# Hybrid decoder layer on one core: one more projection group in seven products, tighter pairs of heads, and 72 convolution taps moved from VectorE to ScalarE and DMAs

## The chip, the cores and the metric

The kernel runs on one core of a Trainium2 chip. The metric is the device time of one execution in microseconds (us). The engines are called as the profile calls them: PE (TensorE, matrix products), DVE (VectorE), ACT (ScalarE), POOL (GpSimd) and SP (SyncE, which here only issues DMAs). Each engine executes its own instructions strictly in the order in which they stand in the program, and waits where an instruction's inputs or its output buffer are not ready.

## The reference

One layer on a sequence of 512 tokens with 2048 channels. The input is normalised and multiplied with a matrix of 7168 columns; the columns feed a causal convolution of 31 taps (mixer A) and an attention with three dilated windows (mixer B); both results are gated and multiplied with the output matrix.

```python
h = rms_norm(x, norm_g)
z = h @ w_in                       # (512, 2048) @ (2048, 7168)
a_val, a_glu, a_gate, q, k, v, b_gate = jnp.split(z, SPLIT_POINTS, axis=-1)

u = a_val * jax.nn.sigmoid(a_glu)
u = causal_depthwise_conv(u, conv_w, conv_b)           # 31 taps
u = jax.nn.silu(layer_norm(u, conv_norm_g, conv_norm_b))
u = u @ conv_pw_w + conv_pw_b
y_a = u * jax.nn.silu(a_gate)

q = rms_norm(q.reshape(bsz, s, N_HEADS, HEAD_DIM), q_norm_g)
k = rms_norm(k.reshape(bsz, s, N_HEADS, HEAD_DIM), k_norm_g)
o = dilated_attention_mixture(q, k, v)
y_b = o.reshape(bsz, s, ATTN_WIDTH) * jax.nn.silu(b_gate)

y = jnp.concatenate([y_a, y_b], axis=-1) @ w_out
return x + y
```

## The kernel before, in words

**Groups, units and slots.** The columns of the matrices are cut into groups of 512. `GROUPS` (line 49) lists them in the order in which PE works on them: four groups `vg` (value and gate of the convolution's GLU), then `q`, `k`, `v`, `bg` (gate of mixer B) of the first eight heads, `q`, `k`, `v` of the other eight, `ag` twice (gate of mixer A), the second `bg`, the convolution's projection `pw` twice, and the output groups `wb` and `wa`. A group's weights come in units of 1 MB (four blocks of 128 rows by 512 columns); a group of the input matrix has four units, a group of `pw` two. The time of the program is counted in slots, eight to a unit; `clock[0]` is the number of the slot that is being written. `vg` 0 to 3 fill slots 0 to 127, `q` 0 slots 128 to 159, `k` 0 slots 160 to 191, the two groups after it slots 192 to 255, `q` 1, `k` 1 and `v` 1 slots 256 to 351, `ag` slots 352 to 415, the second `bg` slots 416 to 447, `pw` slots 448 to 479.

**Three products for one.** Values are kept at higher than fp16 accuracy by splitting each into two fp16 parts. A weight unit of a plain group is split by ACT (`split_hi`, line 297, tile `wh`) and DVE (`split_lo`, line 305, tile `wl`), and each product is three matmuls, high by high, high by low, low by high (`tri`, lines 411 to 415). A plain slot is six matmuls with 512 columns. In a unit with the number i, the `wh` of unit i+1 is issued in its first slot and the `wl` in its third. The pool `parts` holds two units' `wh` and `wl`, so the `wh` of unit i+1 overwrites that of unit i-1 and cannot start before PE has read the last of that unit, at the start of unit i.

**Seven products for eight.** The groups in `SEVEN` (line 54) are done with Winograd's form of Strassen's scheme: the weights and the activations are cut into two by two blocks and seven block products take the place of eight (`input_products`, line 1119, with `ORDER`, line 1116). Such a group has 28 product steps of twelve matmuls with 256 columns in the place of its 32 slots. Block sums of the weights are made by DMAs that POOL issues with `accum_op=add` (line 1134) and by DVE subtractions; each block is split by ACT (`hi`, line 1136) and DVE (`lo`, line 1140); the block products are recombined by ACT copies and DVE additions (`copy`, `joint`, `fourth`, `out`).

**Banks.** The pool `lin_ps` holds four PSUM banks (`LP`, line 32). A plain group uses them for its four row blocks m = 0 to 3. Block m is emptied right after it is done, in slots 1, 3, 5 and 7 of the group's last unit; the next group opens its own block m in slots 0, 2, 4, 6 of its first unit, in the bank of the same m. A gate group (`ag`, `bg`) is emptied by ACT with a Silu (`evac_gate`, line 460).

**The convolution.** `conv` (line 544) works on eight tiles `cv` in pairs. ACT starts each with tap 30 and the bias (line 551), and DVE adds the 30 other taps, each one instruction `cv<-u,cw,cv`. These are fillers: after each slot `run_conv` (line 861) adds DVE instructions of the convolution as long as the counted load of DVE is under a pace per slot (`PACE`, `PACE_2`, in estimated nanoseconds). The sum `lnacc` over the eight tiles, for the LayerNorm's mean, is added up pair by pair as they finish. Three slots after the last addition, PE multiplies it with ones (line 575) and the rest of the LayerNorm follows; its Silu (line 608) and the split of the result into `u16` (line 315) are ACT's.

**Attention.** `attention` (line 800) starts a pair of heads every `PERIOD` slots, eight pairs in all, and `two_heads` (line 706) has the plan of a pair, in slots after its start: scores on PE at 0 and 3, the exponentials of the first head by ACT at 7 and of the second at 11 (`exps`, line 741), their normalised high parts by ACT at 13 and 18 (`high`, line 749) and low parts by DVE at 16 and 21, DMA transposes at 19 and 24, and the products with `v` on PE when the pair ends. With `PERIOD` 32 the eight pairs begin in slots 226, 258, 290, 322, 354, 386, 418 and 450.

**Tables.** ACT needs an `ACT_TABLE_LOAD` when it goes from Exp to Silu or Sigmoid and back; the other functions here (Copy, Identity, Square) need none.

## Time and profile before

| what | us |
|---|---|
| median of 3 runs (815.09 to 815.63) | 815.55 |
| the profiled execution's own time | 815.08 |
| its span, first to last instruction | 813.3 |
| PE busy in it | 806.7 |
| DVE busy | 703.3 |
| ACT busy | 557.5 |
| POOL busy | 132.2 |

The granted TensorE clock was 1.00 over the whole span. The difference between span and time, 1.8 us, lies around the program. A row of the timeline gives start and duration in us, engine, line, operation, tiles and shape; an idle time before it and what ended it stand in brackets. A row such as `x4` merges neighbours. Consecutive instructions of one engine overlap a little (DVE and ACT by 0.08 to 0.1 us, PE by more, since matmuls are pipelined), so the cost of one in a queue is the distance from its start to the next one's start.

### The profile page before, as it was taken

The page shows a single profiled execution, that of the slowest core. Times are in us where ns is not written, and L with a number is a line of the kernel's source. Part 1 is how long each engine was busy: PE and PEld are TensorE (multiplying, and loading weights), DVE is VectorE, ACT ScalarE, POOL GpSimd, SP SyncE. Part 2 cuts the span into 40 slices and gives each one's busy share as a digit, 9 for nine tenths or more (in the row PEclk, how much of TensorE's full clock was granted, in tenths as well). Part 3 has the DMA queues.
Part 4 walks back from the last instruction along what each step waited for, and adds up shares of the span by engine and source line. Part 5 has one row for each costly group of instructions (what it writes and reads, how often), then busy time and mean ns, then how long its engine had stood idle before and what let it go on. Part 6 is the DMA issues. An engine that isn't in the chain of part 4 may idle for free.

```text
span 813.3 us, 13452 instructions
## 1 busy us (share of the span) xinstructions
PE 806.7 (99%) x5271; PEld 500.9 (62%) x5271; DVE 703.3 (86%) x1188; ACT 557.5 (69%) x784; POOL 132.2 (16%) x143
## 2 busy tenths in 40 slices
PE   9999999999999999999999999999999999999998
PEld 6887745888646854444444444444444444788887
DVE  6768999878989989999999989997678798998885
ACT  6667687577756688586757658497688858766540
POOL 0001021322224300004012010000110002412420
PEclk9999999999999999999999999999999999999999
DMA  9852346983874863527474623526352487678752
GB/s 339 329 235 99 109 102 138 142 249 58 311 146 104 149 263 108 122 95 169 142 182 127 150 100 107 123 95 169 104 121 100 137 246 226 118 176 187 130 105 65
DMA packets 98367, 125.60 MB, mean 154 GB/s; under 512 B 62464, under 2 KB 83712, under 8 KB 89088
## 3 DMA queue, kind: packets, MB, share of 16 engines
q1 hardware_dynamic: 80544, 107.37, 42.2%
q0 software_dynamic: 17472, 17.30, 15.0%
q8 instruction: 41, 0.67, 0.3%
q14 instruction: 22, 0.18, 0.1%
q10 hardware_dynamic: 288, 0.07, 0.0%
HBM read 88.56 MB, written 4.19 MB: 114 GB/s over the span
## 4 chain that ended last, share of the span: by engine, by line
PE 90%; DVE 7%; ACT 1%; issue 1%; POOL 0%; DMA 0%; SPq 0%; ACTq 0%; DVEq 0%
PE ps_l L413 24%; PE ps_l L415 23%; PE ps_l L414 23%; PE ps_l L887 10%; DVE cv L81 3%; PE ps_s L413 2%; PE ps_s L415 2%; PE ps_s L414 2%; PE ps_s L730 2%; PE ps_o L771 2%; DVE wl L81 1%; DVE ws L81 1%; ACT junk L191 0%; DVE sx L81 0%; DMA x<-xt_dram 0%
## 5 line engine op out<-in xcount | busy, mean ns | idle before, releaser
L81 DVE SCALAR_TENSOR_TENSOR cv<-u,cw,cv 128x511 f32<-128x511 f32 (+14 forms) x240 | 162.1, 727 | 0.4 <-ACT cv L551 0.4
L191 ACT ACTIVATE junk<-wf 128x2048 uint8<-128x2048 f32 x68 | 129.1, 1899 | 2.4 <-DMA wf<-w_dram 2.1
L300 ACT ACTIVATE wh<-wf,ws 128x2048 f16<-128x2048 f32 x44 | 87.7, 1994 | 52.4 <-PE ps_l L414 50.6
L413 PE MATMUL ps_l<-x,wh 128*128 128x512 f16 x320 | 121.3, 379 | 0.3 <-DVE glu L81 0.3
L415 PE MATMUL ps_l<-x,wl 128*128 128x512 f16 x320 | 121.3, 379 | 0.0
L414 PE MATMUL ps_l<-x,wh 128*128 128x512 f16 x320 | 121.3, 379 | 0.0
L81 DVE SCALAR_TENSOR_TENSOR wl<-wf,ws,wh 128x2048 f16<-128x2048 f32 x45 | 105.6, 2346 | 10.7 <-ACT wh L300 10.7
L413 PE MATMUL ps_l<-wh,x 128*128 128x512 f16 x256 | 97.1, 379 | 0.0
L415 PE MATMUL ps_l<-wh,x 128*128 128x512 f16 x256 | 97.0, 379 | 0.0
L414 PE MATMUL ps_l<-wl,x 128*128 128x512 f16 x256 | 97.0, 379 | 0.0
L81 DVE SCALAR_TENSOR_TENSOR ws<-wf,ws 128x1024 f16<-128x1024 f32 x70 | 89.0, 1278 | 7.1 <-ACT ws L1138 4.5
L413 PEld LDWEIGHTS <-wh 128*128 128x128 f16 x480 | 47.0, 98 | 55.3 <-issue 4.0
L415 PEld LDWEIGHTS <-wl 128*128 128x128 f16 x480 | 46.9, 98 | 53.6 <-DVE wl L81 0.4
L414 PEld LDWEIGHTS <-wh 128*128 128x128 f16 x480 | 46.9, 98 | 50.4 <-issue 0.7
L887 PE MATMUL ps_l<-xr,wr 128*128 128x512 f32 x288 | 69.6, 397 | 0.7 <-ACT xr L338 0.7
L205 POOL TENSOR_SCALAR ws<-ws 128x1 f32<-128x1 f32 x22 | 11.8, 537 | 324.4 <-DVE ws L81 295.6
L887 PEld LDWEIGHTS ps_l<-xr,wr 128*128 128x128 f32 x288 | 53.8, 188 | 14.3 <-ACT xr L338 1.5
L413 PEld LDWEIGHTS <-x 128*128 128x128 f16 x352 | 34.4, 98 | 32.5 <-issue 1.9
L415 PEld LDWEIGHTS <-x 128*128 128x128 f16 x352 | 34.4, 98 | 31.3
L414 PEld LDWEIGHTS <-x 128*128 128x128 f16 x352 | 34.4, 98 | 30.1
L954 ACT ACTIVATE ws<-wf,ws 128x1024 f16<-128x1024 f32 x28 | 32.1, 1147 | 28.3 <-PE ps_l L415 9.7
L1138 ACT ACTIVATE ws<-wf,ws 128x1024 f16<-128x1024 f32 x42 | 47.1, 1138 | 5.8 <-PE ps_l L415 4.8
(251 smaller groups left out, 1816.3 us busy)
## 6 DMA issues: line engine op xcount, KB each, us to landing
wf<-w_dram SPq DMA_DIRECT2D x72, 1024.0 KB, 5.2
wf<-wf POOLq DMA_DIRECT2D x30, 512.0 KB, 6.5
x<-xt_dram SPq DMA_DIRECT2D x16, 256.0 KB, 6.7
res<-xt_dram SPq DMA_DIRECT2D x8, 512.0 KB, 6.6
out_dram<-res SPq DMA_DIRECT2D x15, 256.0 KB, 2.2
wf<-w_dram SPq DMA_DIRECT2D x7, 512.0 KB, 7.2
wf<-wf POOLq DMA_DIRECT2D x6, 256.0 KB, 6.3
wf<-w_dram SPq DMA_DIRECT2D x2, 256.0 KB, 3.1
```

The source lines that it names most:

```text
L81: return getattr(self.engine, name)(out, src, *args, **kw)
L191: A.activation(junk[:, :n], src, AF.Square, scale=scale, accum_out=acc)
L205: G.tensor_scalar(scale, scale, 1e-30, 2.0 ** (-2 * top), op0=OP.max, op1=OP.mult)
L300: A.activation(parts[i][0], raw[i], AF.Copy, scale=wscale[units[i][3:]][0])
L413: T.matmul(ps, ah, bh, start=first, stop=False, skip_group_check=more)
L414: T.matmul(ps, ah, bl, start=False, stop=False, skip_group_check=more)
L415: T.matmul(ps, al, bh, start=False, stop=last, skip_group_check=more)
L730: T.matmul(ps[i, a], qk["q", hf][p4 // 2][rows, p4 % 2, q, i * P:w], qk["k", hf][p4 // 2][rows, p4 % 2, k, :w], start=n == 0, stop=n == 2)
L771: T.matmul(po[rows, i * P:(i + 1) * P], vs[hf][j // 2][:, j % 2, 2 * p4 + a, vp * DH:(vp + 1) * DH], got["t", a][:, pp * (ALL // P) + FROM ...
L887: T.matmul(banks[group, m], wt[:, a, m * P:(m + 1) * P], xk[b], start=k == 0 and a == b == 0, stop=k == KC - 1 and a == 1)
L954: A.activation(t[:, 0], block(name), AF.Copy, scale=wscale["wa", g][0])
L1138: A.activation(t[:, 0], block(name, pair), AF.Copy, scale=wscale[group][0])
```

## The change

1. `bg` 0 stands in front of `v` 0 in `GROUPS`, and is one of the groups in seven products. `input_products` gets a branch that empties such a gate group with Silu.
2. A pair of heads starts every 28 slots instead of 32, and the first 60 slots after `k` 0 instead of 28. The eight pairs now begin in slots 258, 286, 314, 342, 370, 398, 426 and 454. The plan of a pair is shorter: exponentials at 7 and 10, high parts at 11 and 15, low parts at 13 and 17, transposes at 16 and 20.
3. For three of the four pairs of `cv` tiles, 13 of the 31 taps (the starting one and 12 more) are made by ACT into a tile `tap` (two buffers) and summed in DRAM by DMAs that POOL issues with `accum_op=add`, one tap every three slots from slot 70 on, but none while `q` 0 is worked on. When the last has been sent, SP fetches the sum as the start of `cv`, and DVE adds the 18 other taps. So DVE has 72 tap instructions fewer (240 to 168), ACT 72 more, and POOL issues 78 tap DMAs and 6 more block sums for `bg` 0.
4. `lnacc` is added up in one piece, seven additions, when all eight tiles are done. The paces are 1180 and 1370 instead of 1230 and 1480. The pool `slots` has 33 buffers instead of 35.

```diff
-PERIOD = {0: 32, 1: 32}
+PERIOD = 28
-PACE = 1230
+BY_SUMS = {2: 12, 4: 12, 6: 12}
+STEP = 3
+SUMS_FROM = 70
+SLOW = (("q", 0),)
+PACE = 1180
-GROUPS = [... ("q", 0), ("k", 0), ("v", 0), ("bg", 0), ("q", 1), ...
+GROUPS = [... ("q", 0), ("k", 0), ("bg", 0), ("v", 0), ("q", 1), ...
-SEVEN = (("vg", 3), ("q", 0), ("v", 0))
+SEVEN = (("vg", 3), ("q", 0), ("bg", 0), ("v", 0))
-PACE_2 = 1480
+PACE_2 = 1370
+    taps = pool("taps", 2)
+    scratch = pool("scratch", 6, space=bass.MemoryType.DRAM)
+    def tap_sums():
+        for i0, count in BY_SUMS.items():
+            while i0 + 1 not in u:
+                yield 1
+            for i in (i0, i0 + 1):
+                far_sums[i, "at"] = scratch.tile([P, S], F32, name="far")
+            for d in range(count + 1):
+                for i in (i0, i0 + 1):
+                    t = taps.tile([P, S], F32, name="tap")
+                    scale = cw[:, i, TAPS - 1 - d:TAPS - d]
+                    if d == 0:
+                        A.activation(t, u[i], AF.Identity, scale=scale, bias=cb[:, i:i + 1])
+                    else:
+                        A.activation(t[:, d:], u[i][:, :S - d], AF.Copy, scale=scale)
+                    after(1, lambda: nc.gpsimd.dma_start(far_sums[i, "at"][:, d:], t[:, d:],
+                                                         **({"accum_op": OP.add} if d else {})))
+                    yield STEP
+                    while at_group[0] in SLOW:
+                        yield 1
+            far_sums[i0] = far_sums[i0 + 1] = clock[0] + 6
     def conv():
         for i0 in range(0, 8, 2):
+            far = BY_SUMS.get(i0, 0)
+            while far and far_sums.get(i0 + 1, 10 ** 9) > clock[0]:
+                yield 1
             for i in (i0, i0 + 1):
                 cv[i] = slot("cv")
+                if far:
+                    nc.sync.dma_start(cv[i], far_sums.pop((i, "at")))
+                else:
+                    A.activation(cv[i], u[i], AF.Identity, ...)
-            if i0 == 0:
-                acc = slot("lnacc")
-                V.tensor_add(acc, cv[0], cv[1])
-            elif i0 < 6:
-                for i in (i0, i0 + 1):
-                    V.tensor_add(acc, acc, cv[i])
-                    yield 0
         wait[1] = True
-        for i in (6, 7):
+        acc = slot("lnacc")
+        V.tensor_add(acc, cv[0], cv[1])
+        for i in range(2, 8):
             V.tensor_add(acc, acc, cv[i])
         yield 3
-        for a, e in ((0, 7), (1, 11)):
-            h = (13, 18)[a]
+        for a, e in ((0, 7), (1, 10)):
+            h = (11, 15)[a]
-        start = max(clock[0] + 28, ...)
+        start = max(clock[0] + (28 if hf else 60), ...)
```

What this does to the order of the instructions is shown at three places.

The first is ACT between the second `bg` group and `pw` (slots 432 to 447). The names: `wh` is a unit's high part, `cv` a convolution tile in the LayerNorm's Silu, `sx` an exponential, `hl` a high part of the attention weights, `u` the high part of a convolution result, `gate` the emptying of a bank of `bg`, `junk` a sum of squares that measures a weight unit or a gate. In the kernel before, from the `wh` of slot 440 on:

```order
L300 ACTIVATE wh<-wf,ws 128x2048
L608 ACTIVATE cv<-cv,lnb,lng 128x512
L315 ACTIVATE u_6040<-cv,us 128x512
L467 ACTIVATE gate<-ps_l,esc 128x512
L191 ACTIVATE junk,ysumab<-gate 128x512
L608 ACTIVATE cv<-cv,lnb,lng 128x512
L191 ACTIVATE junk,wsum<-wf 128x2048
L315 ACTIVATE u_6073<-cv,us 128x512
L467 ACTIVATE gate<-ps_l,esc 128x512
```

In the changed kernel, in the same stretch, ahead of that `wh`:

```order
L639 ACTIVATE cv<-cv,lnb,lng 128x512
L197 ACTIVATE junk,wsum<-wf 128x2048
L321 ACTIVATE u_6347<-cv,us 128x512
L774 ACT_TABLE_LOAD
L774 ACTIVATE sx,st_6200<-sx,st_6200,sc 128x128
L774 ACTIVATE sx,st_6200<-sx,st_6200,sc 128x256
L774 ACTIVATE sx,st_6200<-sx,st_6200,sc 128x384
L774 ACTIVATE sx,st_6200<-sx,st_6200,sc 128x512
L639 ACT_TABLE_LOAD
L639 ACTIVATE cv<-cv,lnb,lng 128x512
L785 ACTIVATE hl<-sx,st_6199 128x128
L785 ACTIVATE hl<-sx,st_6199 128x256
```

The eight exponentials of a pair (the other head's stand just above, with two table loads of their own) have moved into the stretch of the LayerNorm's Silu, in front of the `wh` of slot 440 and of the four `gate` instructions.

The second place is ACT at the end of the first `ag` group (slots 376 to 383), where `ag` is the emptying of a bank. In the kernel before:

```order
L300 ACTIVATE wh<-wf,ws 128x2048
L467 ACT_TABLE_LOAD
L467 ACTIVATE ag_5132<-ps_l,esc 128x512
L191 ACTIVATE junk,wsum<-wf 128x2048
L467 ACTIVATE ag_5132<-ps_l,esc 128x512
L467 ACTIVATE ag_5173<-ps_l,esc 128x512 x2
```

In the changed kernel, from the second `ag` on:

```order
L473 ACTIVATE ag_5482<-ps_l,esc 128x512
L774 ACT_TABLE_LOAD
L774 ACTIVATE sx,st_5364<-sx,st_5364,sc 128x128
L774 ACTIVATE sx,st_5364<-sx,st_5364,sc 128x256
L774 ACTIVATE sx,st_5364<-sx,st_5364,sc 128x384
L774 ACTIVATE sx,st_5364<-sx,st_5364,sc 128x512
L785 ACTIVATE hl<-sx,st_5363 128x128
L785 ACTIVATE hl<-sx,st_5363 128x256
L321 ACTIVATE y_5523<-gate,yb0s 128x512
L473 ACT_TABLE_LOAD
L473 ACTIVATE ag_5533<-ps_l,esc 128x512
```

The pair that began in slot 370 has its exponentials between the four evacuations, which stood together before; between `wh` and the first `ag` stand the other head's four exponentials and one `y` (the high part of a result of mixer B).

The third place is DVE ahead of the matmul of the LayerNorm's mean (slots 386 to 392). In the kernel before:

```order
L81 SCALAR_TENSOR_TENSOR cv<-u,cw,cv 128x482
L81 TENSOR_SCALAR st_5283<-st_5283 128x4
L81 RECIPROCAL st_5283<-st_5283 128x4
L81 TENSOR_REDUCE ws<-ps_s 128x1
L81 SCALAR_TENSOR_TENSOR cv<-u,cw,cv 128x482
L81 TENSOR_TENSOR lnacc<-lnacc,cv 128x512 x2
```

In the changed kernel, from the `wl` of slot 386 on:

```order
L85 SCALAR_TENSOR_TENSOR wl<-wf,ws,wh 128x2048
L85 SCALAR_TENSOR_TENSOR hl<-sx,st_5364,hl 128x128
L85 SCALAR_TENSOR_TENSOR hl<-sx,st_5364,hl 128x256
L85 TENSOR_SCALAR ws<-ws 128x1
L85 RECIPROCAL wi<-ws 128x1
L85 SCALAR_TENSOR_TENSOR hl<-sx,st_5364,hl 128x384
L85 SCALAR_TENSOR_TENSOR hl<-sx,st_5364,hl 128x512
L85 SCALAR_TENSOR_TENSOR cv<-u,cw,cv 128x484 x2
L85 SCALAR_TENSOR_TENSOR cv<-u,cw,cv 128x483 x2
L85 SCALAR_TENSOR_TENSOR cv<-u,cw,cv 128x482 x2
L85 TENSOR_TENSOR lnacc<-cv 128x512
L85 TENSOR_TENSOR lnacc<-lnacc,cv 128x512 x6
```

Two additions of `lnacc` have become seven, and the whole piece stands behind the `wl` of slot 386. The matmul that reads `lnacc` stands in PE's order in slot 404 before and in slot 395 now, three slots after the last addition in both.

## The prediction

> **What bounds the kernel now.** I read the page's first part, then what PE waited for, then rows of the timeline of PE, ACT and DVE.

> ```profile
> PE 806.7 (99%) x5271; PEld 500.9 (62%) x5271; DVE 703.3 (86%) x1188; ACT 557.5 (69%) x784; POOL 132.2 (16%) x143
> ```

> What PE waited for (total, times, longest, in us):

> ```profile
> PE ps_s L575 <- DVE lnacc L81: 1.0, 1, 1.0
> PE ps_l L413 <- DVE glu L81: 0.3, 1, 0.3
> PE ps_l L414 <- DVE ws L81: 0.2, 1, 0.2
> ```

> PE is busy for 806.7 of 813.3 us, and its only wait in the second half that is worth a name is the 1.0 us for `lnacc`. So the time can fall only by fewer matmuls and by these few waits, and it rises by whatever PE newly waits for. The question is whether ACT and DVE, which feed PE, still meet their due times where the change thickens their queues. What PE's time consists of:

> ```profile
> 212.42 0.38 PE L413 MATMUL ps_l<-wh,x 128*128 128x512 f16 x1
> ...
> 253.88 0.27 PE L413 MATMUL ps_l<-ws,x 128*128 128x256 f16 x1
> ...
> 290.59 0.38 PE L413 MATMUL ps_l<-x,wh 128*128 128x512 f16 x1
> ...
> 588.76 0.38 PE L413 MATMUL ps_l<-x,wh 128*128 128x512 f16 x1
> ...
> 609.53 0.38 PE L413 MATMUL ps_l<-u,wh 128*128 128x512 f16 x1
> ```

> The first matmuls of `k` 0, of the group in seven products after it, and of the group after that: a plain group lasts 253.88 − 212.42 = 41.46 us, one in seven products 290.59 − 253.88 = 36.71. The last two rows are the first matmul of slot 432 and of slot 448: 20.77 us for 16 slots, 1.298 us a slot.

> **The change part by part.**

> *`bg` 0 in seven products.* A plain group becomes one in seven: 41.46 − 36.71 = 4.75 us of PE less, if its feeders keep up. Two such groups stood one behind the other before (`vg` 3, `q` 0), and none of PE's waits above lies there. The gain is −4.75, and 0 at worst.

> *The taps.* 72 instructions leave DVE, and ACT gets 72. From the page the group of the taps and the DMAs of 256 KB (count, size, us to landing):

> ```profile
> L81 DVE SCALAR_TENSOR_TENSOR cv<-u,cw,cv 128x511 f32<-128x511 f32 (+14 forms) x240 | 162.1, 727 | 0.4 <-ACT cv L551 0.4
> ...
> wf<-wf POOLq DMA_DIRECT2D x6, 256.0 KB, 6.3
> ```

> From the view of the waits of the line that issues the accumulating DMAs of the seven groups:

> ```profile
> DMA to landing us min/median/max: 5.5/6.9/11.4
> ```

> And the window of `q` 0 in seven products (length; busy us of PE, PEld, DVE, ACT and POOL; granted clock, DMA share, GB/s):

> ```profile
> 138.70:174.90 36.20, 36.20 (x335) 32.44 (x333) 32.07 (x40) 20.80 (x23) 10.96 (x10) 1.00 0.91 202
> ```

> On DVE that is 72 × 0.727 = 52 us less, which returns no time of its own: DVE is a filler there and PE waited for none of these. (The seven products of `bg` 0 give DVE some of it back.) On ACT a tap is 72 times about 0.70 (the pitch of a 128x512 function, below), 50 us more. A tap's buffer is needed again after two steps of three slots, 6 × 1.298 = 7.8 us; the tap itself takes 0.7 and a DMA of 256 KB 6.3, together 7.0, so ACT doesn't wait at this landing time. In the window ACT is busy for 20.80 of 36.20 us, so 15.4 are free and nine taps (6.3) fit in. DMAs have a share of 0.91 there. At a landing of 11.4 a tap comes only every (0.7 + 11.4) / 2 = 6.05 us instead of 3.9: nine taps hold ACT for 9 × 2.15 = 19 us against 9.1 left free, so the other end is +10. No row shows a case in which DMAs are late as a rule, and the median is 6.9, so I take 0 and keep +10 for a rival. POOL's 84 further issues stand in a queue that is busy for 132.2 of 813.3 us; block sums stand behind tap DMAs there, and what that costs is within the same bounds. SP's six fetches of sums are sent six slots (7.8 us) after the last tap, against a landing of 6.9, and weight fetches stand behind them: a late sum holds them back by up to 11.4 − 7.8 = 3.6 us, which the fetch in advance covers as long as a unit's buffer is ahead.

> *Pairs every 28 slots.* The starts no longer keep their place in the groups, and this is what the kernel pays for. The exponentials of the pair at 370 and of the pair at 426 now stand at slots 377 and 380, and 433 and 436, in ACT's order in front of bank evacuations and of a unit's `wh`. I go through ACT's order with these rows (starts of neighbours; a distance is a price in a queue):

> ```profile
> 577.07 2.00 ACT L300 ACTIVATE wh<-wf,ws 128x2048 f16<-128x2048 f32 x1 [7.09 <-PE ps_l L414]
> 579.09 1.28 ACT L743 ACT_TABLE_LOAD   x1
> 580.38 0.49 ACT L743 ACTIVATE sx<-sx,st,sc 128x128 f32<-128x128 f32 x1
> ...
> 582.95 1.89 ACT L191 ACTIVATE junk<-wf 128x2048 uint8<-128x2048 f32 x1
> ...
> 591.68 1.28 ACT L608 ACT_TABLE_LOAD   x1
> 592.98 0.81 ACT L608 ACTIVATE cv<-cv,lnb,lng 128x512 f32<-128x512 f32 x1
> 593.70 1.89 ACT L191 ACTIVATE junk<-wf 128x2048 uint8<-128x2048 f32 x1
> ...
> 595.59 0.79 ACT L754 ACTIVATE hl<-sx,st 128x128 f16<-128x128 f32 x2
> 596.28 0.80 ACT L608 ACTIVATE cv<-cv,lnb,lng 128x512 f32<-128x512 f32 x1
> 596.99 1.21 ACT L754 ACTIVATE hl<-sx,st 128x384 f16<-128x384 f32 x2
> 598.11 0.71 ACT L315 ACTIVATE u<-cv,us 128x512 f16<-128x512 f32 x1
> 598.72 0.80 ACT L608 ACTIVATE cv<-cv,lnb,lng 128x512 f32<-128x512 f32 x1
> 599.42 0.70 ACT L315 ACTIVATE u<-cv,us 128x512 f16<-128x512 f32 x1
> 600.03 1.99 ACT L300 ACTIVATE wh<-wf,ws 128x2048 f16<-128x2048 f32 x1
> 601.93 0.80 ACT L608 ACTIVATE cv<-cv,lnb,lng 128x512 f32<-128x512 f32 x1
> ...
> 613.91 0.67 ACT L467 ACTIVATE gate<-ps_l,esc 128x512 f32<-128x512 f32 x1
> ```

> A table load is 592.98 − 591.68 = 1.30; `wh` 601.93 − 600.03 = 1.90; a head's four exponentials 582.95 − 580.38 = 2.57; `junk` 1.89; a Silu of `cv` 0.70; `u` or `y` 0.61; the two small `hl` 0.69, the two large 1.12; an evacuation 0.57 (its 0.67 less the 0.1 of overlap). The first row says that `wh` had been held for 7.09 us by a PE matmul: it overwrites the tile that PE reads until its unit ends. That fixes a point of departure: in slots 376 and 432, each a unit's first, ACT cannot have begun its `wh` before PE is there, however early it was idle.

> *Slots 432 to 448, T = 0 at slot 432.* ACT in order: `wh` 1.90, `cv` 2.60, load 3.90, exponentials 6.47, `u` 7.08, load 8.38, `cv` 9.08, `junk` 10.97, `u` 11.58, load 12.88, exponentials 15.45, load 16.75, `cv` 17.45, `hl` 18.14, `u` 18.75, `hl` 19.87, `cv` 20.57, `u` 21.18, `wh` of slot 440 23.08, `hl` 23.77, `u` 24.38, first `gate` 24.95. PE wants that bank for `pw` in slot 448, at 20.77. So 4.2 us is the least that it waits. Behind the ACT `gate` stand on DVE, in this order, the product `gate` and the `wl` of `pw`'s first unit:

> ```profile
> 605.76 0.75 DVE L81 SCALAR_TENSOR_TENSOR gate<-opair,osc,gate 128x512 f32<-128x512 f32 x1 [1.64 <-ACT gate L467]
> 606.43 2.35 DVE L81 SCALAR_TENSOR_TENSOR wl<-wf,ws,wh 128x2048 f16<-128x2048 f32 x1
> ```

> Before, they ended at 606.43 + 2.35 = 608.78, 1.2 us ahead of what PE reads third in slot 448. Now: 24.95 + 0.67 + 2.35 = 27.97, and PE's third matmul wants it at 20.77 + 0.43 = 21.2. PE waits 6.8 us in all. What ACT does there without the eight exponentials and four loads takes 24.95 − 5.14 − 5.2 = 14.6, so nothing else is late.

> *Slots 376 to 395, T = 0 at slot 376.* ACT: `wh` 1.90, exponentials 4.47, `y` 5.08, load 6.38, `ag` 6.95, `junk` 8.84, `y` 9.45, `ag` 10.02, load 11.32, exponentials 13.89, `hl` 14.58, `y` 15.19, load 16.49, third `ag` 17.06, `hl` 18.18, `y` 18.79, `ag` 19.36, `wh` 21.26. PE opens the third bank in slot 388, at 12 × 1.298 = 15.58, and waits 1.5. The `wl` behind that `wh` ends at 21.26 + 2.35 = 23.6, while PE wants it in slot 392, at 22.7 with the wait before: 0.9 more, say 0.8 for its rounding.

> *`lnacc` in one piece.* On DVE behind that `wl`:

> ```profile
> 538.87 5.12 DVE L81 SCALAR_TENSOR_TENSOR cv<-u,cw,cv 128x486 f32<-128x486 f32 x8
> 543.92 0.16 DVE L81 TENSOR_SCALAR st<-st 128x4 f32<-128x4 f32 x1
> 544.88 1.41 DVE L81 TENSOR_TENSOR lnacc<-lnacc,cv 128x512 f32<-128x512 f32 x2
> 546.21 0.74 DVE L81 SCALAR_TENSOR_TENSOR hl<-sx,st,hl 128x128 f16<-128x128 f32 x2
> 546.87 2.34 DVE L81 SCALAR_TENSOR_TENSOR wl<-wf,ws,wh 128x2048 f16<-128x2048 f32 x1
> 549.13 1.27 DVE L81 SCALAR_TENSOR_TENSOR hl<-sx,st,hl 128x384 f16<-128x384 f32 x2
> ```

> `wl` has a pitch of 549.13 − 546.87 = 2.26, a tap here (543.92 − 538.87) / 8 = 0.63, an addition of `lnacc` (546.21 − 544.88) / 2 = 0.665, the two small `hl` 0.66, the two large 1.18 (1.27 less overlap). From 21.26: `wl` 23.5, then 0.66 + 0.25 (two tiny ones) + 1.18 + 6 × 0.63 + 7 × 0.665 = 10.5, done at 34.1. PE comes to the mean's matmul in slot 395 at 19 × 1.298 + 2.3 = 26.96, and everything behind that matmul waits with it: 7.1 us. Were DVE free of ACT's lateness it would come to about 15.58 + 10 = 26, with nothing to wait for; so this term lies between 0 and 7.1, and I take 7.1 because each step in it has a row. The 1.0 us of the old wait goes.

> *The paces, `slots` with 33 buffers, the shorter plan of a pair* have no price of their own: they only shift fillers on DVE, whose load falls. The three table loads more than before are in the walks.

> **The sum:** 815.08 (the profiled execution, span 813.3 and 1.8 around it, 0.06% below the median) − 4.75 − 1.0 + 9.4 (1.5 + 0.8 + 7.1) + 6.8 = 825.5 us. The two walks add up, since each starts from a `wh` that PE itself releases.

> [...]

> **The rivals.**

> - *ACT is not late (faster).* If the queue in front of the first `gate` is done by 20.77 instead of 24.95, and that of slot 376 by 15.58 instead of 17.06, PE waits only as before: 815.08 − 4.75 − 1.0 + 0.2 = 809.5. It would need pieces of the walk to be cheaper by a sixth. For it: before, ACT was idle for 7.09 us in front of a `wh`, so it has slack elsewhere; against: `wh` ties the walk to PE, and its prices are the rows above. 0.15.
> - *Only one place is late.* Without the `lnacc` term's 7.1 it is 818.4; without the 6.8 it is 818.7; without the whole 9.4, 816.1: about 817.5. 0.17.
> - *The taps get in the way.* The ACT tap waits for its buffer, and behind it stand the block splits of `bg` 0 and `v` 0. It decides where the landing goes over 7.8 − 0.7 = 7.1, close to the median of 6.9. Between 0 and +10, at the share of 0.91 some +6 on top of the sum: 831.5. 0.15.
> - *A switch of tables costs more than its load.* If each change between Exp and Silu held ACT for as long again as its load, some 1.3 us, three loads in the one walk and four in the other make it 825.5 + 9 = 834.6. The rows show no such time. [...] 0.03.

> **How the numbers follow.** The forecast has 0.50. A measurement of this kernel can tell about 0.2%, 1.6 us. The first rival lies under that (faster 0.15), a little of the second falls below or within it (0.01 and 0.06); the rest is slower: faster 0.16, same 0.06, slower 0.78. The range goes from 815 (the second rival with small waits) to 834 (the taps' rival at most of its price); the first rival and the dearest ends are left out, 0.18. For the forecast alone, with 4.2 to 6.8 at the second place and 5 to 7.1 for `lnacc`, it is 820 to 827.

> **What would show it.** Right: PE waits of about 7 us with `lnacc` ahead of the mean's matmul, 4 us or more on ACT's `gate` and then on `wl` before `pw`, one of 1 to 2 us on `ag`; `bg` 0 lasting 36.7 us; ACT without a gap between slots 432 and 441. Wrong: ACT idle in front of the second `wh` there; PE waits in `bg` 0 or `v` 0 behind a `tap`; an Exp that starts well over 1.3 us after its table load; a PE that stays at 99% busy.

## The result and the profile after

| | before | after |
|---|---|---|
| median, us | 815.32 (4 runs, 815.05 to 815.63) | 920.93 (4 runs, 918.22 to 928.21) |
| profiled execution, span, us | 813.3 | 917.1 |
| PE busy, us | 806.7 | 831.5 |
| mean granted clock of PE | 1.00 | 0.959 |

The ratio is 1.131 (95% interval 1.124 to 1.138): 13% slower, 103.8 us in the spans. The prediction had 825.5 us and a range up to 834. From the page of the kernel after, the engines:

```profile
PE 831.5 (91%) x5415; PEld 524.1 (57%) x5415; DVE 673.1 (73%) x1132; ACT 614.3 (67%) x878; POOL 199.0 (22%) x228
```

What PE waited for in it (total, times, longest, us):

```profile
PE ps_o L802 <- DMA pt<-hl: 18.7, 4, 10.3
PE ps_l L419 <- ACT ws L1172: 16.3, 3, 9.5
PE ps_l L419 <- ACT cb L1222: 8.6, 3, 3.6
PE ps_s L606 <- DVE lnacc L85: 7.2, 1, 7.2
PE ps_l L421 <- DVE ws L85: 6.9, 7, 1.6
PE ps_l L419 <- ACT gate L473: 4.6, 1, 4.6
PE ps_s L400 <- DVE lnacc L85: 3.3, 1, 3.3
PE ps_l L421 <- DVE wl L85: 2.9, 2, 2.1
PE ps_l L420 <- DVE wl L85: 2.7, 2, 2.4
PE ps_l L419 <- ACT ag L473: 1.8, 1, 1.8
```

The waits that the prediction names are all there: 1.8 for `ag`, 7.2 for `lnacc`, 4.6 for `gate`, then `wl`. But at the top stand others: DMA transposes (`pt`), and the block splits `ws` and copies `cb` of the groups in seven products. What ACT waited for shows where those come from, and the view of the line that issues the tap DMAs shows how long these took:

```profile
ACT tap L566 <- DMA far<-tap: 75.5, 24, 9.9
```

```profile
DMA to landing us min/median/max: 2.4/5.2/20.1
```

ACT stood for 75.5 us in front of a tap whose buffer a DMA still held. These DMAs landed after 5.2 us in the median, and after up to 20.1. To find the place, I count matmuls in PE's order and take the time from the first one of a slot to the first of a later slot:

| slots | before, us | after, us | difference |
|---|---|---|---|
| 0 to 96 | 133.5 | 134.0 | +0.5 |
| 96 to 160 (`vg` 3, `q` 0) | 73.8 | 91.9 | +18.1 |
| 160 to 192 (`k` 0) | 41.5 | 41.6 | +0.1 |
| 192 to 256 (`v` 0 and `bg` 0) | 80.2 | 100.5 | +20.3 |
| 256 to 352 (`q`, `k`, `v` 1) | 136.0 | 169.6 | +33.6 |
| 352 to 384 | 45.3 | 45.3 | 0 |
| 384 to 480 (`ag` 1, `bg` 1, `pw`) | 139.5 | 169.5 | +30.0 |
| 480 to the end | 158.4 | 159.6 | +1.2 |

72 us lie in slots 96 to 352, where taps are sent, and 30 behind slot 384, where the prediction had its stalls. In the windows view (length; busy us of PE, PEld, DVE, ACT, POOL; clock, DMA share, GB/s), `vg` 3, then `bg` 0, then `v` 0 in the kernel after:

```profile
139.18:183.02 43.84, 37.62 (x338) 32.39 (x337) 32.44 (x41) 27.74 (x36) 17.88 (x20) 1.00 1.00 182
...
272.62:319.38 46.76, 39.40 (x338) 33.07 (x338) 33.83 (x44) 32.90 (x44) 26.82 (x25) 0.96 1.06 149
319.38:373.09 53.71, 40.31 (x340) 34.17 (x337) 31.00 (x36) 33.44 (x43) 15.27 (x18) 0.87 1.01 226
```

The DMA share is 1.00 and over, at only 149 GB/s in `bg` 0, where `vg` 3 had 0.91 at 202 GB/s before. (That row of the prediction, from 138.70 to 174.90 us, is called the window of `q` 0 there, but slot 96, where `vg` 3 begins, starts at 138.63 us; `q` 0 had 0.66 at 155 GB/s. By the plan taps are sent in `vg` 3 and not in `q` 0, so it is the right row under a wrong name.) How that reaches PE is seen at 318 to 338 us. ACT:

```profile
323.02 1.13 ACT L1172 ACTIVATE ws<-wf,ws 128x1024 f16<-128x1024 f32 x1
334.01 0.72 ACT L566 ACTIVATE tap<-u,cw 128x506 f32<-128x506 f32 x1 [9.86 <-DMA far<-tap]
...
336.53 1.13 ACT L1172 ACTIVATE ws<-wf,ws 128x1024 f16<-128x1024 f32 x1
```

POOL:

```profile
313.85 0.89 POOL L567 DMA_DIRECT2D far<-tap  x1 [0.95 <-ACT tap L566]
319.25 0.86 POOL L567 DMA_DIRECT2D far<-tap  x1 [4.51 <-ACT tap L566]
327.79 1.30 POOL L1168 DMA_DIRECT2D wf<-wf  x1 [7.67 <-DMA wf<-wf]
```

and PE:

```profile
337.71 0.37 PE L419 MATMUL ps_l<-ws,x 128*128 128x256 f16 x1 [9.51 <-ACT ws L1172]
```

The tap at 334.01 waits 9.86 us for its buffer, which the DMA issued at 313.85 has held for 20 us. Behind it in ACT's order stands the `ws` of 336.53, and PE waits 9.51 us for that. Meanwhile POOL's block sum at 327.79 waits 7.67 us for an earlier block sum: the weights' own DMAs are late too. Issued from 275 to 375 us, nine fetches of a weight unit from DRAM land after 9.0 us in the median; in the same two groups before (254 to 334 us) nine took 5.5. And the six transposes `pt` issued from 400 to 530 us land after 7.3 to 10.8 us, where those before took 4.8 to 8.2; PE's 18.7 us of waiting for them stand at the top of its list.

The third part of the page gives packets, MB and share of all 16 engines' span of each queue; `q0` is POOL's, with the accumulating DMAs, `q1` that of the weights. Before:

```profile
q1 hardware_dynamic: 80544, 107.37, 42.2%
q0 software_dynamic: 17472, 17.30, 15.0%
```

And after:

```profile
q0 software_dynamic: 31488, 40.66, 30.1%
```

15.0% of 813.3 us is 122 us, 30.1% of 917.1 is 276. Of the 154 us more, the six additional block sums of 512 KB take 22 (the 36 before, 33 times 512 KB in bytes, took 122), so by this estimate a tap's DMA fills all engines for (154 − 22) / 78 = 1.7 us. One every three slots (3.9 us) adds 0.44 to a share of 0.9. By bytes, 23.36 MB in 154 us are 152 GB/s, where the weights' 107.37 MB in 42.2% of 813.3 us have 313.

**The stretch behind slot 384.** In front of `pw`, in ACT, DVE and PE:

```profile
681.86 2.00 ACT L306 ACTIVATE wh<-wf,ws 128x2048 f16<-128x2048 f32 x1 [1.70 <-PE ps_l L420]
...
703.52 1.99 ACT L306 ACTIVATE wh<-wf,ws 128x2048 f16<-128x2048 f32 x1
...
706.72 0.67 ACT L473 ACTIVATE gate<-ps_l,esc 128x512 f32<-128x512 f32 x1
```

```profile
707.51 0.74 DVE L85 SCALAR_TENSOR_TENSOR gate<-opair,osc,gate 128x512 f32<-128x512 f32 x1
708.17 2.34 DVE L85 SCALAR_TENSOR_TENSOR wl<-wf,ws,wh 128x2048 f16<-128x2048 f32 x1
```

```profile
707.43 0.59 PE L419 MATMUL ps_l<-u,wh 128*128 128x512 f16 x1 [4.62 <-ACT gate L473]
...
710.58 0.61 PE L421 MATMUL ps_l<-u,wl 128*128 128x512 f16 x1 [2.13 <-DVE wl L85]
```

ACT begins the first `gate` at 706.72, 24.86 us after the `wh` of slot 432 (681.86); the walk had its end at 24.95, its start at 24.38. `gate` and `wl` on DVE follow as said, and PE waits 4.62 and 2.13 us. What the walk lacks is the clock. Windows around the wait for `lnacc`:

```profile
601.00:605.00 4.00, 3.19 (x16) 1.49 (x16) 3.97 (x9) 3.97 (x4) 0.00 (x0) 1.00 0.64 167
605.00:609.00 4.00, 0.45 (x3) 0.00 (x0) 3.95 (x7) 1.89 (x2) 0.00 (x0) 1.00 1.07 279
609.00:611.00 2.00, 0.00 (x0) 0.00 (x0) 1.91 (x3) 0.11 (x2) 0.00 (x0) 0.97 0.00 0
611.00:617.00 6.00, 4.33 (x8) 1.57 (x9) 3.81 (x4) 0.60 (x1) 0.00 (x0) 0.50 0.21 37
617.00:620.00 3.00, 3.00 (x13) 1.18 (x11) 0.00 (x0) 0.00 (x0) 0.00 (x0) 0.88 0.66 276
```

PE stands from 605.5 to 612.7, and the granted clock drops to 0.50 from 610.9 to 617.7: in PE's first 5.0 us of work after the wait a matmul of 512 columns comes every 0.43 us, and behind them every 0.22. Summed over windows of 1 us, PE's busy time multiplied by what is missing of the clock is 23.1 us in the whole kernel (0 before), 7.8 of it behind slot 384 after three waits.

### The profile page after: what moved, and what is told of

Same layout as the page of the kernel before. It is cut to its first block, busy times and chain, and to the rows that moved or that the text cites. A ratio compares the mean times of both kernels' runs of the same rounds, so it can differ in the third digit from the quotient of the medians.

```text
span 917.1 us, 13995 instructions
## 1 busy us (share of the span) xinstructions
PE 831.5 (91%) x5415; PEld 524.1 (57%) x5415; DVE 673.1 (73%) x1132; ACT 614.3 (67%) x878; POOL 199.0 (22%) x228
## 3 DMA queue, kind: packets, MB, share of 16 engines
q0 software_dynamic: 31488, 40.66, 30.1%
## 4 chain that ended last, share of the span: by engine, by line
PE 44%; DMA 20%; ACT 13%; DVE 11%; issue 7%; POOL 3%; SPq 0%; ACTq 0%; POOLq 0%; DVEq 0%
DMA far<-tap 15%; PE ps_l L921 9%; PE ps_l L419 9%; PE ps_l L420 9%; PE ps_l L421 9%; DMA pt<-hl 4%; ACT sx L774 3%; DVE wl L85 3%; ACT junk L197 2%; ACT wh L306 2%; PE ps_o L802 2%; PE ps_s L421 2%; PE ps_s L419 2%; POOL wf L1168 2%; PE ps_s L420 2%
## 5 line engine op out<-in xcount | busy, mean ns | idle before, releaser
L85 DVE SCALAR_TENSOR_TENSOR ws<-wf,ws 128x1024 f16<-128x1024 f32 x84 | 107.1, 1279 | 41.0 <-ACT ws L1172 38.3
L85 DVE SCALAR_TENSOR_TENSOR wl<-wf,ws,wh 128x2048 f16<-128x2048 f32 x41 | 96.3, 2348 | 39.4 <-ACT wh L306 39.4
L567 POOL DMA_DIRECT2D far<-tap x78 | 70.7, 910 | 222.9 <-ACT tap L566 153.9
L85 DVE SCALAR_TENSOR_TENSOR cv<-u,cw,cv 128x499 f32<-128x499 f32 (+19 forms) x168 | 113.7, 725 | 1.0 <-ACT cv L587 1.0
L566 ACT ACTIVATE tap<-u,cw 128x511 f32<-128x511 f32 (+11 forms) x72 | 50.9, 708 | 75.5 <-DMA far<-tap 75.5
L419 PE MATMUL ps_l<-x,wh 128*128 128x512 f16 x256 | 99.0, 387 | 2.1 <-ACT ag L473 1.8
L421 PE MATMUL ps_l<-x,wl 128*128 128x512 f16 x256 | 98.6, 385 | 0.8 <-DVE wl L85 0.8
L420 PE MATMUL ps_l<-x,wh 128*128 128x512 f16 x256 | 98.7, 386 | 0.0
L306 ACT ACTIVATE wh<-wf,ws 128x2048 f16<-128x2048 f32 x40 | 79.7, 1992 | 23.3 <-PE ps_l L420 22.5
L419 PEld LDWEIGHTS <-wh 128*128 128x128 f16 x416 | 41.3, 99 | 53.7 <-issue 8.0
L420 PEld LDWEIGHTS <-wh 128*128 128x128 f16 x416 | 41.0, 99 | 48.4 <-issue 6.6
L1172 ACT ACTIVATE ws<-wf,ws 128x1024 f16<-128x1024 f32 x56 | 63.2, 1136 | 0.6 <-DMA wf<-wf 0.6
## 6 DMA issues: line engine op xcount, KB each, us to landing
x<-xt_dram SPq DMA_DIRECT2D x16, 256.0 KB, 6.6
out_dram<-res SPq DMA_DIRECT2D x15, 256.0 KB, 2.2
far<-tap POOLq DMA_DIRECT2D x6, 256.0 KB, 3.2
cv<-far SPq DMA_DIRECT2D x6, 256.0 KB, 5.2
```

Of the source, the lines that this page charges most:

```text
L85: return getattr(self.engine, name)(out, src, *args, **kw)
L306: A.activation(parts[i][0], raw[i], AF.Copy, scale=wscale[units[i][3:]][0])
L419: T.matmul(ps, ah, bh, start=first, stop=False, skip_group_check=more)
L420: T.matmul(ps, ah, bl, start=False, stop=False, skip_group_check=more)
L421: T.matmul(ps, al, bh, start=False, stop=last, skip_group_check=more)
L566: A.activation(t[:, d:], u[i][:, :S - d], AF.Copy, scale=scale)
```

## The experiments

Theory A: the tap DMAs overload the 16 DMA engines, and ACT's wait for their buffers brings that to PE; behind slot 384 it is the pairs' exponentials and table loads, as predicted, with the clock on top. Rivals: ACT's own longer queue (B), DVE's debt (C), the two buffers and POOL's order, whatever the size of the DMAs (D). Eleven kernels were run. Times are medians of runs, or one run where no ratio stands beside them, against 815.2 to 815.4 for the kernel before on the same chip. Runs of one kernel with stalls lie up to 10 us apart (918.2 to 928.2 for the kernel after), so smaller differences are read from slots and waits of the traces.

**1. No taps.** `BY_SUMS` empty, and paces that keep the LayerNorm's place:

```diff
-BY_SUMS = {2: 12, 4: 12, 6: 12}
+BY_SUMS = {}
-SLOTS = 33
+SLOTS = 35
-PACE = 1180
+PACE = 1340
-PACE_2 = 1370
+PACE_2 = 1520
```

> No taps by ACT and DMA: DVE adds all 240 taps again (paces 1340 and 1520, so that the mean's matmul stands one slot from where it stands in the changed kernel; 35 buffers in slots). Bg 0 in seven products, the pairs every 28 slots and lnacc in one piece stay. Theory A (the tap DMAs overload the 16 DMA engines, whose share is 1.00, 0.96, 1.06 and 1.01 in the four stretches from slot 112 to 256): PE's waits before slot 352 vanish, both seven groups last about 36.7 us without the attention's own matmuls, and only what came behind slot 352 stays: 815.3 - 4.75 + 30.9 = 841 us. Theory B (ACT's longer queues and the tighter pairs by themselves slow the stretch from slot 96 to 352, the DMAs are incidental): over 880 us, since only 50 us of ACT's 66 go. Theory C (DVE, with 72 taps and the work of bg 0 back, is the bound in the place of the DMAs): 850 to 880 us, with PE waiting for DVE's wl and ws.

Measured: 860.37 us, ratio 1.0554 (1.0514 to 1.0595). 60 us go, but 841 is not reached, so A doesn't hold alone; the size is C's. PE's waits in it:

```profile
PE ps_s L606 <- DVE lnacc L85: 9.1, 1, 9.1
PE ps_l L419 <- ACT gate L473: 5.4, 2, 4.7
PE ps_l L420 <- DVE ws L85: 3.5, 4, 1.3
```

The wait for `lnacc` grows from 7.2 to 9.1, and slots 192 to 256 take 80.8 us instead of 73.4.

**2. Taps made by ACT, but 72 of the 78 DMAs left out.**

```diff
-                    after(1, lambda: nc.gpsimd.dma_start(far_sums[i, "at"][:, d:], t[:, d:],
-                                                         **({"accum_op": OP.add} if d else {})))
+                    if d == 0:
+                        after(1, lambda: nc.gpsimd.dma_start(far_sums[i, "at"][:, d:], t[:, d:]))
```

> ACT makes all 78 taps as in the changed kernel, but only the first of each tile is sent to DRAM; the other 72 DMAs are left out, so those taps are missing from the sum. Theory A (DMA engines): the stretch to slot 352 loses its waits, 838 to 846 us. Theory B (ACT's own 50 us for the taps, in front of the block splits): it stays over 880 us, and PE still waits for ws in the seven groups.

Measured: 856.6 us, 64 less than the changed kernel. Slots 96 to 160 take 74.3 us (91.9 with the DMAs; 73.8 before), and slots 192 to 256 81.2 (100.5). B falls for these 64 us: ACT makes every tap here. 11 us over A's number stay.

**3. The same DMAs, written plainly.**

```diff
-                    after(1, lambda: nc.gpsimd.dma_start(far_sums[i, "at"][:, d:], t[:, d:],
-                                                         **({"accum_op": OP.add} if d else {})))
+                    after(1, lambda: nc.gpsimd.dma_start(far_sums[i, "at"][:, d:], t[:, d:]))
```

> All 78 tap DMAs are sent, with the same bytes, but written plainly and not added up in DRAM, so that only the last tap of each tile is kept. Theory A1 (it is the read and add in DRAM that costs the DMA engines so much: the accumulating queue moved 23.4 MB more for 30.1% x 917 - 15.0% x 813 = 154 us of all 16 engines, 152 GB/s, against 313 GB/s on the queue of the weights): the share in the seven groups falls under 0.95 and the time to 850 to 875 us. Theory A2 (any 256 KB more every three slots is too much): 890 to 925 us. Theory D (it is not the engines but the two tap buffers and the order of POOL's queue): 900 to 925 us, with ACT still waiting over 60 us for far.

Measured: 889.89 us, between A1 and A2, on the edge of A2, though the share in `vg` 3, `bg` 0 and `v` 0 is 0.88, 0.92 and 0.89, under the 0.95 of A1. The queue and ACT's wait, which is under the 60 us of D:

```profile
q0 software_dynamic: 25728, 40.66, 22.3%
```

```profile
ACT tap L566 <- DMA far<-tap: 45.1, 17, 8.9
```

The same 40.66 MB take 22.3% of 888.1 us, 198 us instead of 276, and the kernel is 31 us faster. So about half of the 64 us is the adding in DRAM, and the other half comes with plain DMAs too.

**4. `lnacc` pair by pair,** with 1's other edits (paces 1380 and 1520):

```diff
-        acc = slot("lnacc")
-        V.tensor_add(acc, cv[0], cv[1])
-        for i in range(2, 8):
+            if i0 == 0:
+                acc = slot("lnacc")
+                V.tensor_add(acc, cv[0], cv[1])
+            elif i0 < 6:
+                ...
+        for i in (6, 7):
             V.tensor_add(acc, acc, cv[i])
```

> As no_taps, with lnacc added pair by pair again (paces 1380 and 1520 bring the mean's matmul to two slots from its place). By my walk the wait of 7.2 us in front of the mean's matmul goes, and with it the half-speed clock behind it (about 7 us at 0.50, 2.6 us lost once PE runs again): 8 to 10 us less than no_taps. Rival: DVE is late there because of ACT's late wh, whatever the number of additions; then it is only the five additions less, 3.3 us.

Measured: 863.02 us, beside 857.5 to 864.7 for 1. The wait shrinks only from 9.1 to 4.9:

```profile
PE ps_s L611 <- DVE lnacc L85: 4.9, 1, 4.9
```

That is nearer to the rival (3.3). The time doesn't fall: PE's waits are 3.0 us less in sum (36.8 against 39.8), but half clock takes 15.4 us of its work, by the sum used above, where it took 9.7 in 1. That DVE is late because ACT's `wh` and so `wl` are, as the rival has it, is argued from their order and not tested.

**5. The pairs alone,** in the kernel before:

```diff
-PERIOD = {0: 32, 1: 32}
+PERIOD = {0: 28, 1: 28}
-        for a, e in ((0, 7), (1, 11)):
-            h = (13, 18)[a]
+        for a, e in ((0, 7), (1, 10)):
+            h = (11, 15)[a]
-        start = max(clock[0] + 28, ...)
+        start = max(clock[0] + (28 if hf else 60), ...)
...
```

> The kernel before with the pairs of heads alone changed: every 28 slots, the first 60 after k 0, the shorter plan; no taps, bg 0 plain, lnacc pair by pair. If the exponentials and table loads in front of wh, ag and gate are what costs the stretch behind slot 376 (theory of the prediction's walks), PE waits about 1.5 to 2 us on ag, 1 us on wl, 4.7 and 2.5 us on gate and wl in front of pw, and at the mean up to 7, each longer wait with 2 to 3 us of half clock behind it: 832 to 846 us. Rival: the stretch is slow because bg 0 in seven products and the paces leave DVE in debt: then the pairs alone cost under 8 us, 815 to 823 us.

Measured: 836.81 us, ratio 1.0262 (1.0247 to 1.0278), as the walks' theory has it. The places are partly others, as the LayerNorm stands 17 slots later here than in the changed kernel:

```profile
PE ps_s L203 <- DVE st L81: 3.7, 2, 3.0
PE ps_l L413 <- ACT u L315: 3.6, 1, 3.6
PE ps_l L413 <- ACT ag L467: 1.8, 1, 1.8
```

`ag` is as predicted (1.8); in front of `pw` PE waits for ACT's `u`, not for `gate`.

**6. The taps alone:** the changed kernel with groups, `SEVEN` and pairs of before.

```diff
-PERIOD = 28
+PERIOD = 32
-... ("bg", 0), ("v", 0), ("q", 1) ...
+... ("v", 0), ("bg", 0), ("q", 1) ...
-SEVEN = (("vg", 3), ("q", 0), ("bg", 0), ("v", 0))
+SEVEN = (("vg", 3), ("q", 0), ("v", 0))
...
```

> The changed kernel with groups, SEVEN and pairs as before (bg 0 plain and behind v 0, pairs every 32 slots with the old plan): of the change there are left the taps, the paces and lnacc in one piece. If the tap DMAs overload the DMA engines whatever the rest of the schedule, the time is 60 to 75 us over the kernel before, 875 to 890 us, with a DMA share near 1.0 in the third group vg and in v 0 and PE waits there. Rival: only together with bg 0 in seven products is it too much; then 830 to 850 us.

Measured: 889.73 us, 74.5 over before, at the upper end of what A gives. `vg` 3 takes 46.9 us and `v` 0 49.0, where both took 36.7, at DMA shares of 0.99 and 1.03. But not all of the 74.5 is A's. 12.4 us lie behind slot 352, where no tap is sent (the paces and `lnacc` in one piece are left in this kernel). And in `bg` 0 PE waits 7.6 us for a `gate` that waits for a small product on POOL, of which 10 has a second case:

```profile
364.11 11.90 POOL L432 TENSOR_TENSOR esc<-wi,xinv 128x1 f32<-128x1 f32 x1
```

That leaves at most 54 us, a little under what A gives and far over the 15 to 35 of the rival. The rival falls: the taps need no help from the other edits.

**7. Identity in the place of Exp,** otherwise as 1:

```diff
-            A.activation(xi, xi, AF.Exp, ...)
+            A.activation(xi, xi, AF.Identity, ...)
```

> As no_taps, with Identity in the place of Exp (the attention's weights are wrong), so that ACT needs no table loads for the attention. By the walks ACT's queue in front of pw shrinks by four loads, 5.2 us, to 19.75 of 20.77 us, so gate isn't waited for and wl only 1 to 2 us; in slots 376 to 392 it shrinks by 3.9, and the wait for ag goes: 12 to 20 us under no_taps (860.4), 840 to 848. Rival: the loads stand beside other waits and give 0 to 5 us.

Measured: 846.84 us, 13.5 under 1. PE no longer waits for `gate` or `ag`, and for `wl` once 1.6 us (the walk: 22.8 − 21.2):

```profile
PE ps_l L421 <- DVE wl L85: 1.6, 1, 1.6
PE ps_s L606 <- DVE lnacc L85: 8.4, 1, 8.4
```

So the table loads are what makes ACT late in front of `pw`. The wait for `lnacc` hardly shrinks (9.1 to 8.4): there DVE's own queue counts.

**8. The tap DMAs with 64 columns** in the place of up to 511:

```diff
-                    after(1, lambda: nc.gpsimd.dma_start(far_sums[i, "at"][:, d:], t[:, d:],
+                    w = S if d == 0 else d + 64
+                    after(1, lambda: nc.gpsimd.dma_start(far_sums[i, "at"][:, d:w], t[:, d:w],
```

> The changed kernel with the same 78 tap DMAs, buffers and order on POOL, but each accumulating DMA sends 64 columns in the place of up to 511 (the rest of those taps is missing from the sum). If it is the bytes that fill the DMA engines, the time comes near to the kernel without these DMAs (856.6): 856 to 868 us, ACT's wait for far under 15 us of 75.5. If it is the two buffers and POOL's order, the round trip of a DMA however small, it stays over 885 us.

Measured: 880.28 us, between the two:

```profile
ACT tap L566 <- DMA far<-tap: 43.0, 17, 6.4
```

By the spans, 917.1 − 878.5 = 38.6 us go with the bytes, and 878.5 − 854.7 = 23.8 only with the DMAs as such. But small DMAs take time of the engines too. POOL's queue in 2, then here:

```profile
q0 software_dynamic: 21120, 22.02, 17.3%
...
q0 software_dynamic: 31488, 24.39, 21.1%
```

17.3% of 854.7 us is 148 us, and 21.1% of 878.5 is 185: the 72 small DMAs take 37 us of all engines. In 3 the plain ones take 50, in the changed kernel the accumulating ones 128. Over 2, the spans are longer by 23.8, 33.4 and 62.4 us, in the same order. So the loss grows with the engine time of the DMAs, as A has it, though less than in proportion. How much of the 23.8 us is D's, the two buffers and POOL's order, stays open: no kernel was run with more buffers for the taps.

**9. The taps left out altogether** (the convolution lacks them):

```diff
-    convolution, sums_of_taps = conv(), tap_sums()
+    convolution, sums_of_taps = conv(), iter(())
...
-            yield 4 if far else 2
+            yield 2
```

> The changed kernel with the 72 taps simply left out: neither ACT nor DMAs nor DVE make them (the convolution lacks them), so this is what the rest of the change would be if they cost nothing. In no_taps slots 192 to 256 took 80.8 us where the seven products of bg 0 should leave 73.4. If DVE's debt was the cause, they take 73.4 to 75 here, and the time is pairs_only 836.8 - 4.75 + 8.7 for lnacc in one piece (64.85 - 56.13, slots 384 to 416 of the changed kernel and of pairs_only) = 841 us. Rival: two groups in seven products behind one another, with ACT and POOL loaded as they are, are late by themselves: 80 us there and 847 to 855 us.

Measured: 845.63 us. Slots 192 to 256 take 74.9 us, with one wait of 1.2 us:

```profile
PE ps_l L420 <- DVE ws L85: 1.2, 1, 1.2
```

So DVE's debt was why 1 lost the gain of `bg` 0. The total is 4.6 us over the expectation, 3.8 of them in slots 416 to 448 (54.3 us, 50.4 in 5), which the sum left out.

**10. Taps for one pair of tiles, outside the seven products:** as 6, with

```diff
-BY_SUMS = {2: 12, 4: 12, 6: 12}
+BY_SUMS = {6: 12}
-SUMS_FROM = 70
-SLOW = (("q", 0),)
+SUMS_FROM = 140
+SLOW = (("vg", 3), ("q", 0), ("v", 0))
-PACE = 1180
+PACE = 1210
-PACE_2 = 1370
+PACE_2 = 1440
```

> The changed kernel with groups, SEVEN and pairs as before, and with taps for one pair of tiles only (24 off DVE), sent outside the groups in seven products: 11 in k 0, the others in bg 0 and q 1, paces 1210 and 1440. K 0 has a DMA share of 0.61 before and had no wait with taps in the changed kernel either (41.59 us). If only DMA engines that are full make taps dear, this costs nothing to speak of and, DVE being no bound, gains nothing: 813 to 818 us. Rival: taps in plain groups cost too (ACT in front of wh, transposes behind weights): 825 to 835 us.

Measured: 852.69 us, ratio 1.0468 (1.0442 to 1.0495): worse than both. `k` 0, in which ten tap DMAs are sent, takes 42.1 us (41.5 before), which fits A; slots 192 to 256 lose 12.4 us and slots 384 to 448 21.4. The largest loss in the first is not a DMA's:

```profile
335.71 11.14 POOL L432 TENSOR_TENSOR esc<-wi,xinv 128x1 f32<-128x1 f32 x1
```

```profile
339.59 7.21 DVE L85 SCALAR_TENSOR_TENSOR cv<-u,cw,cv 128x500 f32<-128x500 f32 x11
```

```profile
346.88 0.69 ACT L473 ACTIVATE gate<-ps_l,esc 128x512 f32<-128x512 f32 x1 [10.74 <-POOL esc L432]
```

A product of two 128x1 tiles on POOL, behind a tap's issue, takes 11.14 us, until 346.85, which is when a row of eleven DVE taps ends (346.80) and DVE, after working without a pause since 327.45, stands idle. ACT's `gate` waits 10.74 us for it, and PE 7.7. The loss behind slot 384 shows in waits for `lnacc` (3.8), the LayerNorm's `diag` (2.9), `wh` (3.1) and `wl` (3.3); whether the paces or `lnacc` in one piece brought them isn't shown. So this kernel is no clean test of DMAs with room; that question stays open.

**11. One slot more before the mean's matmul,** in the kernel before:

```diff
             V.tensor_add(acc, acc, cv[i])
-        yield 3
+        yield 4
```

> The kernel before with four slots in the place of three between the last addition of lnacc and the matmul of the mean. The one wait of 1.0 us that PE has there goes: 814.4 us, 0.12% less. Rival: what follows (the LayerNorm, later by one slot) has no slack either: the same time or more.

Measured: 814.07 us, ratio 0.9985 (0.9977 to 0.9994). The wait for `lnacc` is gone from PE's list. It is about a microsecond under the kernel before.

## Why the prediction was wrong, point by point

- **`bg` 0 in seven products** (−4.75): wrong in the changed kernel, where the two groups take 100.5 us. Without the taps (9) they take 74.9 where before, less the 2.1 us of scores that the later pairs took out of these slots, they took 78.2: −3.3. That no wait lay in two such groups was read from a trace in which ACT was busy for 20.80 us of one (`vg` 3) and 26.32 of the other; in `bg` 0 it is 32.90, with 75.5 us of waiting beside it in the whole kernel.
- **The taps** (0, at most +10): this is the step that failed. By the spans of 9, 2 and the changed kernel they cost 917.1 − 843.9 = 73 us: 11 with ACT's 78 instructions and the first DMA of each tile (854.7 − 843.9), and 62 with the other 72 DMAs. The step set the landings of the kernel before (6.3, at worst 11.4) against the 7.8 us until the buffer is needed, as if its own DMAs would not change them. It had the DMA share of 0.91 in the row and didn't add to it what it was about to send. 1.7 us of all engines every 3.9 us would make it 0.91 + 0.44 = 1.35, and no group of the kernel after has more than 1.06. The median landing of the taps, 5.2 us, is even under the 7.1 at which the prediction saw the danger; but 24 of the 72 taps met a buffer that was still held, by landings of up to 20.1. And the bound of +10 counted nine taps of one group, though taps run from slot 70 to 338: the attention's transposes (18.7 us of PE's waits) weren't thought of. The rival on the taps had the mechanism and a seventh of its size at most; the prediction's own sign of being wrong, PE waits in `bg` 0 or `v` 0 behind a `tap`, is the one that the trace shows. How the 62 us divide between ACT's wait for buffers and the late DMAs of weights and transposes stays open.
- **Slots 376 to 395 and 432 to 448** (1.5, 0.8, 7.1; 4.2 growing to 6.8): right, to 0.5 us a term: by the waits 1.8, 0.8 (`wl`, the smaller of its two), 7.2, and 4.62 + 2.13 = 6.75. 7 shows the loads as the cause of the one at `gate`.
- **What comes behind these waits** (no term in the sum): wrong. The second sum of the LayerNorm waits 3.3 us for `lnacc`, and three waits bring half clock, 7.8 us. So 30.0 us came where 15.2 were forecast (9.4 + 6.8 − 1.0).
- **The paces and the shorter plan have no price**: not shown. The pairs with their plan alone cost 21.6 us (5), where the terms of the walks without `lnacc` come to 9.1; 5.7 are half clock by the same sum over windows, and part of the rest lies at places that no walk covered (`u` in front of `pw`, `st` ahead of a small sum on PE). No run has the plan or the paces alone.
- **A switch of tables costs its load alone**: right. In the kernel after, an Exp starts 1.29 us after the start of its load (684.59, 685.88), and the load 0.02 us after the end of the `cv` ahead of it. The load lasts 1.28 us, so 0.03 us are left around it for anything more.

## What to carry to other kernels

Before sending DMAs from a kernel, work out how long one fills all DMA engines (bytes by the rate that its own kind reaches here: 152 GB/s for the accumulating ones of this change, 313 for weights) and add that to the DMA share that the stretch has without them: in `bg` 0 and `v` 0, which have shares of 0.94 and 0.86 in 2 and got 0.44 on top by the estimate above, other DMAs were late too, not only the new ones (weight fetches 9.0 us instead of 5.5). What that costs depends on who waits. `k` 0, with a share of 0.61 before, lost 0.1 us; slots 256 to 352, with 0.49 to 0.56 before, lost 33.6, and 18.7 of it are PE's waits right behind the late transposes. An engine that waits for the buffer of such a DMA hands the delay to all that stands behind it in its order (ACT's 9.86 us became 9.51 of PE), so a filler of this kind doesn't belong on an engine that also feeds the bottleneck. And a stall of PE was dearer than its length where half clock came with it, ten times in the kernel after: by 1.4 to 3.4 us each time.
